# Layer 1 of a two-layer encoder trunk: the merge of the head groups goes by way of DRAM instead of transposes, and two sets of operands start at other addresses

## The chip, the cores and the metric

The kernel runs on one core of one Trainium2 chip. The metric is the device time of one execution in microseconds (us); it is measured several times, and the median is given. TensorE (PE) multiplies and transposes, VectorE (DVE) and ScalarE (ACT) compute elementwise, GpSimd (POOL) does a little elementwise work, and SyncE (SP) issues most of the loads.

## What is computed

The input is one sequence of 512 tokens with 1024 numbers each. Two layers follow each other, each an attention and a SwiGLU FFN with RMSNorm ahead of both, and a last RMSNorm. Layer 0 has windowed attention with grouped queries and is touched by the change only in the address of two buffers. Layer 1 is dilated attention: three groups of 16 heads look at their own token's neighbourhood at steps of 1, 4 and 16, and for every head the three outputs are added with weights that come from the three softmax denominators.

```python
DILATED_GROUPS = ((128, 1), (512, 4), (2048, 16))
BLOCK_B = 64

def dilated_mixture_attention(h, w_qkv, w_out):
    b, s, _ = h.shape
    qkv = (h @ w_qkv).reshape(b, s, N_GROUPS_B, 3, H_B, HEAD_DIM)
    slopes = alibi_slopes(H_B)[:, None]
    outs, lses = [], []
    for gi, (win, dil) in enumerate(DILATED_GROUPS):
        q = to_residue(qkv[:, :, gi, 0], dil)[:, :, :, None]
        k = to_residue(qkv[:, :, gi, 1], dil)
        v = to_residue(qkv[:, :, gi, 2], dil)
        o, lse = banded_attention(q, k, v, slopes, dil, win // (2 * dil), BLOCK_B)
        outs.append(from_residue(o[:, :, :, 0], b, dil))
        lses.append(from_residue(lse[:, :, :, 0], b, dil))
    wts = jax.nn.softmax(jnp.stack(lses), axis=0)
    o = jnp.einsum('gbsh,gbshd->bshd', wts, jnp.stack(outs).astype(jnp.float32))
    return o.astype(h.dtype).reshape(b, s, H_B * HEAD_DIM) @ w_out
```

## The kernel before

All values are fp32. For a matmul each operand is split into a high part, rounded for TensorE (names that end in h), and the rest (names that end in l), and `mm3` (L113 to L119) runs three products: high by high, high by low, low by high. Each is a matmul of a 128x128 weight tile with 256 moving columns. The normed input stands feature by token in xh and xl, the attention output in oh and ol, the hidden part of the FFN in ah and al.

**Weights.** `unit` (L161) is a product of all 512 tokens with 128 weight columns: 8 steps of six matmuls. `values` (L190) makes the values of four heads, tokens by columns, with the input as stationary and the weights as moving operand, and its accumulator is named psv. A weight block of 128x1024 comes by a DMA from SP into wraw (L101), and `split` (L91) makes wh on ScalarE (L92) and wl on VectorE (L93). There are three buffers of each (pool wpool).

**Order of the work.** TensorE's order is written by hand (`manual_schedule`). In layer 1 the matmuls of the projections are the filler: `fillers` yields steps of six matmuls, and `weave` puts a given number of them (32, 48 at the first) between the steps of a list which attention returns. The instructions of the other engines are put in order by a scheduler from modelled times, so an instruction that waits holds up all that was put behind it on its engine. PSUM has eight banks: mm 3, sc 2, tp 2, ov 1; a step that asks for a bank waits until its last user is through.

**Layer 1.** Eight head pairs p of two heads follow each other. For each, `attention_a` does group 0 (step 1) and `attention_b` groups 1 and 2 together, by residue class c of four. The queries and keys of group 0 are qa and ka (L585, L595), split into qs, ks and kl (`split_queries`, `split_keys`); those of the next pair are made as filler while this pair's attention_b runs, and its `scores_a` (L639) needs them.

1. `scores_a` makes the scores of four query tiles, and VectorE and ScalarE turn them to weights not yet divided. Per query and head they leave two numbers, minus the maximum and the sum of exponentials, in sta, a tile of 128 queries by 4 tiles by 32 columns of which 4 are used.
2. `merge_turn` (L763) transposes sta on TensorE (L766), and five copies on VectorE (L771) put the statistics into strow in the order of the classes. `merge_back` (L779) transposes strow back with four small transposes (L781) and copies the result to sa (L784): the statistics of the same queries, in the order which attention_b uses.
3. `turn_a` and `weigh_a` transpose the weights (L661) and multiply by the values (L680). The sum goes to acca, 128 (two heads of 64 features) by 512 queries.
4. `scores_b` makes the scores of groups 1 and 2 for two classes at a time (L698), takes the maximum with sa's (L714), the exponentials, and the common denominator. From these comes the share that group 0 has per query and head; L726 spreads it over 64 columns into ew.
5. `turn_b` transposes the weights: the first half on TensorE (L740), the second on VectorE (L743, pt from pr). `merge_rows` (L786) transposes the four parts of ew on TensorE (L790), so that the share stands in a row for every feature, and multiplies acca by it (L792).
6. `weigh_b` multiplies by the values (L753), adds acca (L759, tmp) and splits into oh and ol for this pair.

At the end `out_part` runs the output projection from oh and ol: five of its eight blocks run alone behind the last attention, after three that serve as the last filler.

In these loops, `bank("tp")` serves the transposes of turn_a, turn_b and of all three merge functions. GpSimd has no instruction in layer 1 from the first operands to the end of attention.

Of the kernel before, what the change touches and what calls it, by code (L numbers as in the profile page):

```python
# [12 lines left out]
OP = mybir.AluOpType  # L13
# [51 lines left out]
def trunk(ctx, tc, xT, gains, sink, tabs, qsc, wunits, wv, outT):  # L65
# [29 lines left out]
    def weight_tiles():  # L95
        return (wpool.tile([128, 1024], F32, name="wraw"), wpool.tile([128, 1024], F32R, name="wh"),
                wpool.tile([128, 1024], F32R, name="wl"))

    def load(tiles, src, cols):
        raw, wh, wl = (t[:, cols] for t in tiles)  # L100
        nc.sync.dma_start(raw, src[:, cols])  # L101
        split(wh, wl, raw)

    def chunks(tiles, shape):
        n = int(np.prod(shape))
        return [t[:, :n].rearrange("p (a b) -> p a b", a=shape[0]) for t in tiles[1:]]

    def load_unit(src, shape):
        tiles = weight_tiles()
        load(tiles, src, slice(0, int(np.prod(shape))))  # L110
        return chunks(tiles, shape)
# [77 lines left out]
    def values(i, col, hi, lo, out, tags="mm mm mm mm"):  # L189


        def gen():
            w = [load_unit(wv[2 * i + k], (4, 256)) for k in range(2)]
# [104 lines left out]
    with tc.tile_pool(name="l0", bufs=2) as pool:  # L298
        v0 = pool.tile([128, 4, 256], F32, name="v0", bufs=1)
        pool.tile([128, 96], F32, name="align", bufs=1)  # L300
# [260 lines left out]
    with tc.tile_pool(name="l1", bufs=2) as pool:  # L561
        pool.tile([128, 96], F32, name="align", bufs=1)
# [4 lines left out]

        stats = [pool.tile([128, 4, 32], F32, name=f"sta{k}", bufs=1) for k in range(2)]
        for t in stats:
            nc.gpsimd.memset(t, 0.0)  # L570
# [51 lines left out]
        def scores_a(p, ts):  # L622
            if ts[0] == 0:
                st["sta", p] = stats[p % 2]
# [62 lines left out]
        def scores_b(p, cs):  # L687
# [28 lines left out]
            for c in cs:  # L716
                for a in range(2):
# [6 lines left out]
            ew = pool.tile([128, 2, 2, 64], F32, name="ew", bufs=3)  # L724
            st["ew", p, cs[0]] = ew
            nc.vector.tensor_tensor(ew, e[:, :, :, None].to_broadcast([128, 2, 2, 64]),  # L726
                                    den[:, :, :, None].to_broadcast([128, 2, 2, 64]), op=OP.mult)
# [35 lines left out]
        def merge_turn(p):  # L763

            ps = bank("tp", "stt")
            nc.tensor.transpose(ps[:, :128], st["sta", p].rearrange("p t e -> p (t e)"), ident)  # L766
            row = st["row", p] = pool.tile([4, S], F32, name="strow", bufs=1)
            by_class = row.rearrange("p (m i) -> p i m", m=16)

            def put(i, n, src):  # L770
                nc.vector.tensor_copy(by_class[:, i:i + n], src.rearrange("p (i m) -> p i m", m=16))  # L771

            put(0, 4, ps[:4, 64:128])
# [187 lines left out]
```

## Time and profile before

| what | value |
|---|---|
| median of 3 runs | 1470.56 us (1470.53 to 1471.1) |
| the profiled execution | 1470.28 us |
| its span, first to last instruction | 1468.5 us |
| granted TensorE clock, mean | 0.994 |
| matmuls and transposes (PE) | 12820 |
| VectorE's and ScalarE's instructions | 1400 and 1126 |
| DMA | 128.29 MB, mean 87 GB/s |

The span is the profiler's time from the first to the last instruction of one execution; the execution as a whole is 1.8 us longer. Lines of the page's groups read: line, engine, operation, output from inputs, shape and count, then busy time and the mean ns of one, then the idle time ahead of it and what ended most of it. Lines of the timeline read: start and duration in us, engine, line, operation, output from inputs, shape, and how many alike; in brackets the wait ahead of it, and on what. A matmul's duration runs to its modelled end, so matmuls overlap, and what one costs TensorE is the distance between two starts. Lines of stretches read: from and to, their length, then busy time and count of TensorE, of the weight loads, VectorE, ScalarE and GpSimd, then the granted clock, the DMA engines' busy share and GB/s.

### The profile page before, as it was taken

To read this page: it belongs to the slowest core of one execution; us is meant where nothing else is said; L and a number is where in the kernel's file an instruction comes from. 1 tells how busy PE (TensorE), PEld (TensorE's weight loads), DVE (VectorE), ACT (ScalarE), POOL (GpSimd) and SP (SyncE) were. 2 spreads that over 40 slices of the span, in tenths; PEclk is the share of its full clock that TensorE was granted. 3 is DMA by queue.
4 is the path that set the end of the run, shared out by engine and by line. 5 is a ranking of instruction groups with operands and counts; after the bars stand their busy time and mean duration, and the time that the engine had idled before them with its cause. 6 is when DMAs were issued, how large, how long until landed. Compare 5 with 4: busy or idle time off the path is not lost.

```text
span 1468.5 us, 29609 instructions
## 1 busy us (share of the span) xinstructions
PE 1451.2 (99%) x12820; PEld 1424.3 (97%) x12820; DVE 732.6 (50%) x1400; ACT 612.0 (42%) x1126; POOL 110.7 (8%) x152
## 2 busy tenths in 40 slices
PE   8999999999999999999999999999999999999997
PEld 8988999999999999999999999999999999999997
DVE  6776544444443345346556556556464444443223
ACT  6776433322323335444545536536343332332221
POOL 4334200000000010000000000000030000000111
PEclk9999999999999999999999999999999999999998
DMA  6110222233223232312212122122132233232321
GB/s 202 58 59 15 87 101 87 101 101 98 93 91 105 94 100 77 109 58 91 82 59 87 65 80 84 61 87 73 44 116 90 98 101 101 87 101 91 97 102 58
DMA packets 38450, 128.29 MB, mean 87 GB/s; under 512 B 4528, under 2 KB 6832, under 8 KB 38320
## 3 DMA queue, kind: packets, MB, share of 16 engines
q1 hardware_dynamic: 36832, 125.08, 25.6%
q8 instruction: 100, 1.64, 0.4%
q10 hardware_dynamic: 1488, 1.33, 0.3%
q14 instruction: 30, 0.25, 0.1%
HBM read 124.29 MB, written 2.10 MB: 86 GB/s over the span
## 4 chain that ended last, share of the span: by engine, by line
PE 94%; DVE 2%; ACT 2%; issue 0%; DMA 0%; POOL 0%; DVEq 0%; SPq 0%; ACTq 0%; POOLq 0%
PE mm L118 52%; PE sc L118 16%; PE psv L118 9%; PE tp L118 8%; PE sc L698 1%; PE ov L379 1%; PE sc L639 1%; PE sc L140 1%; PE ov L753 1%; PE tp L365 1%; PE tp L661 1%; PE ov L680 1%; PE tp L740 0%; DVE wl L93 0%; DVE x L475 0%
## 5 line engine op out<-in xcount | busy, mean ns | idle before, releaser
L92 ACT ACTIVATE wh<-wraw 128x1024 fp32r<-128x1024 f32 (+3 forms) x239 | 247.0, 1035 | 599.3 <-PE mm L118 253.8
L93 DVE TENSOR_TENSOR wl<-wraw,wh 128x1024 fp32r<-128x1024 f32 (+3 forms) x239 | 290.5, 1216 | 201.4 <-ACT wh L92 200.7
L118 PE MATMUL mm<-xh,wh 128*128 128x256 f32 x1632 | 330.7, 284 | 0.9 <-ACT xh L217 0.9
L118 PE MATMUL mm<-xh,wl 128*128 128x256 f32 x1632 | 321.2, 278 | 1.4 <-DVE wl L93 1.4
L118 PE MATMUL mm<-xl,wh 128*128 128x256 f32 x1632 | 321.3, 278 | 0.3 <-DVE xl L218 0.3
L118 PEld LDWEIGHTS mm<-xh,wh 128*128 128x128 f32 x1632 | 248.2, 189 | 6.7 <-issue 4.8
L118 PEld LDWEIGHTS mm<-xh,wl 128*128 128x128 f32 x1632 | 248.2, 189 | 1.9 <-DVE wl L93 1.8
L118 PEld LDWEIGHTS mm<-xl,wh 128*128 128x128 f32 x1632 | 248.3, 189 | 0.9 <-DVE xl L218 0.7
L232 POOL TENSOR_TENSOR ssum<-ssum,tmp 128x512 f32<-128x512 f32 x34 | 54.7, 1609 | 991.3 <-ACT tmp L228 976.7
L118 PE MATMUL psv<-wh,xh 128*128 128x256 f32 x288 | 82.6, 287 | 0.0
L118 PE MATMUL psv<-wh,xl 128*128 128x256 f32 x288 | 80.3, 279 | 0.0
L118 PE MATMUL psv<-wl,xh 128*128 128x256 f32 x288 | 80.2, 279 | 0.0
L118 PE MATMUL mm<-al,wh 128*128 128x256 f32 x374 | 74.8, 276 | 0.0
L118 PE MATMUL mm<-ah,wh 128*128 128x256 f32 x374 | 74.8, 277 | 0.0
L118 PE MATMUL mm<-ah,wl 128*128 128x256 f32 x374 | 74.6, 276 | 0.0
L118 PE MATMUL tp<-xh,wh 128*128 128x256 f32 x352 | 68.8, 277 | 0.0
L118 PE MATMUL tp<-xh,wl 128*128 128x256 f32 x352 | 68.8, 276 | 0.0
L118 PE MATMUL sc<-xh,wh 128*128 128x256 f32 x352 | 68.7, 277 | 0.0
L118 PE MATMUL tp<-xl,wh 128*128 128x256 f32 x352 | 68.6, 276 | 0.0
L118 PE MATMUL sc<-xh,wl 128*128 128x256 f32 x352 | 68.6, 276 | 0.0
L118 PE MATMUL sc<-xl,wh 128*128 128x256 f32 x352 | 68.5, 276 | 0.0
L118 PE MATMUL sc<-al,wh 128*128 128x256 f32 x330 | 66.1, 276 | 0.0
(175 smaller groups left out, 2726.4 us busy)
## 6 DMA issues: line engine op xcount, KB each, us to landing
wraw<-wunits SPq DMA_DIRECT2D x192, 512.0 KB, 3.2
wraw<-wv SPq DMA_DIRECT2D x26, 512.0 KB, 3.2
wraw<-wunits SPq DMA_DIRECT2D x16, 384.0 KB, 2.9
x<-xT SPq DMA_DIRECT2D x8, 256.0 KB, 5.2
wraw<-wunits SPq DMA_DIRECT2D x3, 256.0 KB, 5.4
outT<-x ACTq DMA_DIRECT2D x2, 384.0 KB, 2.7
tab<-tabs SPq DMA_DIRECT2D x1, 512.0 KB, 5.7
outT<-x ACTq DMA_DIRECT2D x2, 256.0 KB, 2.2
```

What stands on the lines that cost most here:

```text
L92: nc.scalar.activation(out_h, src, AF.Copy)
L93: nc.vector.tensor_tensor(out_l, src, out_h.bitcast(F32), op=OP.subtract)
L118: nc.tensor.matmul(out[:, cols], a, b[:, cols], start=first and k == 0 and c == 0, stop=last and k == 2, skip_group_check=True)
L140: nc.tensor.matmul(outs[a], qp[a][:, qc], k[a][:, kc], start=first and k is kp, stop=k is low, skip_group_check=True)
L232: nc.gpsimd.tensor_tensor(norm["sum"], norm["sum"], sq, op=OP.add)
L365: nc.tensor.transpose(tp[:, 256 * hf + 128 * i:256 * hf + 128 * i + 128], st["pr"][:, 2 * i + hf, 128 * kb:128 * kb + 128], ident)
L379: nc.tensor.matmul(ov[64 * hf:64 * hf + 64, :256], v0[:, k0 // 128 + kb, vs], st["pt", kb][:, 256 * hf:256 * hf + 256], start=(kb == 0), s ...
L639: nc.tensor.matmul(out, qk["qs", p][a][:, 128 * t:128 * t + 128], kp[k], start=t == ts[0] and k == 0, stop=k == 1, skip_group_check=True)
L661: nc.tensor.transpose(tp[:, (nb * a + kb) * 128:(nb * a + kb) * 128 + 128], st["pr", p, ts][:, a, o + 128 * kb:o + 128 * kb + 128], ident)
L680: nc.tensor.matmul(ov[rows, 128 * t - 64:128 * t + 64], v[:, t - 1 + kb, vs], pt[:, 256 * a + 128 * kb:256 * a + 128 * kb + 128], start=Fa ...
L698: nc.tensor.matmul(ps[a][:, o:o + 128], qk["q", p, 1 + g][rows, cols], qk["k", p, 1 + g][rows, cols], start=(o == 0), stop=True, skip_grou ...
L753: nc.tensor.matmul(ov[rows, 128 * c:128 * c + 128], vals[p // 2, 1 + g][:, c, hv + 64 * a:hv + 64 * a + 64], pts[g][:, 256 * a + 128 * (c ...
```

## The change

It has two parts.

**The merge of the groups.** `merge_turn` and `merge_back` are replaced by `merge`: GpSimd stores sta (now 128x4x4, a new tile for each pair) to a DRAM tile stats of 512 queries and 64 more, which hold the first 64 again, by two DMAs, and loads sa from it by four, each 32 partitions, in the order of the classes. L726's wide product becomes a small one, 128x4; after each half of scores_b GpSimd stores the shares of both heads to a DRAM tile (two DMAs with pieces of 4 bytes, L727 after the change), and `merge_rows` loads each head's row of 512 shares to 64 partitions (two DMAs, L780 after the change). The multiplication with acca is now `weigh_rows` (L783 after the change), which reads SBUF rather than PSUM and is called one pause later. The transposes on TensorE and the copies on VectorE go. The step at which `merge` is called stands ahead of the first turn rather than behind the second.

**Addresses.** The filler tile align is 64 floats rather than 96 in both layers, so oh and ol start 128 bytes earlier, at 448 rather than 64 modulo 512 bytes. The tiles wh and wl are 1152 columns wide rather than 1024, and the weights of values start 96 floats into them, at 384 rather than 0 modulo 512; other weights stay at 0.

```diff
     def weight_tiles():
-        return (wpool.tile([128, 1024], F32, name="wraw"), wpool.tile([128, 1024], F32R, name="wh"),
-                wpool.tile([128, 1024], F32R, name="wl"))
-
-    def load(tiles, src, cols):
-        raw, wh, wl = (t[:, cols] for t in tiles)
+        return (wpool.tile([128, 1024], F32, name="wraw"), wpool.tile([128, 1152], F32R, name="wh"),
+                wpool.tile([128, 1152], F32R, name="wl"))
+
+    def load(tiles, src, cols, at=0):
+
+        raw, wh, wl = tiles[0][:, cols], *[t[:, at + cols.start:at + cols.stop] for t in tiles[1:]]
...
-            w = [load_unit(wv[2 * i + k], (4, 256)) for k in range(2)]
+            w = [load_unit(wv[2 * i + k], (4, 256), 96) for k in range(2)]
...
-        pool.tile([128, 96], F32, name="align", bufs=1)
+        pool.tile([128, 64], F32, name="align", bufs=1)
...
-
-        stats = [pool.tile([128, 4, 32], F32, name=f"sta{k}", bufs=1) for k in range(2)]
-        for t in stats:
-            nc.gpsimd.memset(t, 0.0)
+        dram = ctx.enter_context(tc.tile_pool(name="dram", bufs=2, space=bass.MemoryType.DRAM))
...
-                st["sta", p] = stats[p % 2]
+
+                st["sta", p] = pool.tile([128, 4, 4], F32, name="sta")
...
-            ew = pool.tile([128, 2, 2, 64], F32, name="ew", bufs=3)
-            st["ew", p, cs[0]] = ew
-            nc.vector.tensor_tensor(ew, e[:, :, :, None].to_broadcast([128, 2, 2, 64]),
-                                    den[:, :, :, None].to_broadcast([128, 2, 2, 64]), op=OP.mult)
+            if cs[0] == 0:
+                st["shares", p] = dram.tile([2, S], F32, name="shares")
+            nc.vector.tensor_tensor(e, e, den, op=OP.mult)
+            for a in range(2):
+                nc.gpsimd.dma_start(st["shares", p][a].rearrange("(c p) -> p c", c=4)[:, both], e[:, :, a])
...
-        def merge_turn(p):
...
+        def merge(p):
+
+
+            sta = st["sta", p]
+            by_query = dram.tile([S + 64, 4], F32, name="stats")
+            nc.gpsimd.dma_start(by_query[:S].rearrange("(t q) e -> q t e", t=4), sta)
+            nc.gpsimd.dma_start(by_query[S:], sta[:64, 0, :])
 
             sa = st["sa", p] = pool.tile([128, 4, 4], F32, name="sa")
-            nc.vector.tensor_copy(sa.rearrange("p c e -> p (c e)"), ps[:, :16])
+            by_class = by_query[64:].rearrange("(m c i) e -> i m c e", c=4, i=4)
+            for i in range(4):
+                nc.gpsimd.dma_start(sa[32 * i:32 * i + 32], by_class[i])
 
         def merge_rows(p):
 
-            pr = bank("tp", "rrow")
-            for c in range(4):
-                nc.tensor.transpose(pr[:, 128 * c:128 * c + 128],
-                                    st["ew", p, c // 2 * 2][:, c % 2].rearrange("p a d -> p (a d)"), ident)
-            nc.vector.tensor_tensor(st["acca", p], pr, st["acca", p], op=OP.mult)
+            rows = st["rows", p] = pool.tile([128, S], F32, name="rows", bufs=1)
+            for a in range(2):
+                nc.gpsimd.dma_start(rows[HALVES[a]], st["shares", p][a:a + 1].to_broadcast([64, S]))
+
+        def weigh_rows(p):
+            nc.vector.tensor_tensor(st["acca", p], st["rows", p], st["acca", p], op=OP.mult)
...
             return [lambda: scores_a(p, (0, 1)), 0, lambda: scores_a(p, (2, 3)), 0,
-                    lambda: turn((0, 1), 0), lambda: turn((0, 1), 1), lambda: merge_turn(p),
-                    lambda: turn((2, 3), 2), 0, lambda: turn((2, 3), 3), lambda: merge_back(p), 0, weigh]
+                    lambda: merge(p), lambda: turn((0, 1), 0), lambda: turn((0, 1), 1),
+                    lambda: turn((2, 3), 2), 0, lambda: turn((2, 3), 3), 0, 0, weigh]
...
             return [lambda: scores_b(p, (0, 1)), pauses[0], 0, lambda: scores_b(p, (2, 3)), pauses[1], 0, 0,
-                    lambda: turn((0, 1)), pauses[2], 0, 0, lambda: turn((2, 3)), pauses[3], lambda: merge_rows(p),
-                    pauses[4], 0, weigh]
+                    lambda: turn((0, 1)), pauses[2], 0, 0, lambda: turn((2, 3)), pauses[3],
+                    lambda: merge_rows(p), pauses[4], lambda: weigh_rows(p), weigh]
```

Three places show how the instructions move. The first is VectorE in the second half of pair 2, behind the last product that makes the shares. Names: wl is a weight block's low part, pt the transposed weights of attention, qa, qs and ka the next pair's queries and keys, mm their accumulator. Before:

```order
L726 TENSOR_TENSOR ew<-mb 128x256
L93 TENSOR_TENSOR wl<-wraw,wh 128x1024
L743 STREAM_TRANSPOSE pt_8922<-pr_8768 128x512
L93 TENSOR_TENSOR wl<-wraw,wh 128x1024
L585 SCALAR_TENSOR_TENSOR qa<-mm,qs_sb,rb 128x16x28
L585 SCALAR_TENSOR_TENSOR qa<-mm,qs_sb,rb 128x16x4
L743 STREAM_TRANSPOSE pt_8982<-pr_8833 128x512
L93 TENSOR_TENSOR wl<-wraw,wh 128x1024
L128 TENSOR_TENSOR qs_8975<-qa,qs_8975 64x512
L128 TENSOR_TENSOR qs_8976<-qa,qs_8976 64x512
L792 TENSOR_TENSOR acca<-rrow,acca 128x512
L595 TENSOR_TENSOR ka<-mm,rb 128x16x32
```

The same place after:

```order
L725 TENSOR_TENSOR mb<-mb 128x4
L93 TENSOR_TENSOR wl<-wraw,wh 128x1024
L743 STREAM_TRANSPOSE pt_8907<-pr_8750 128x512
L93 TENSOR_TENSOR wl<-wraw,wh 128x1024
L783 TENSOR_TENSOR acca<-rows,acca 128x512
L583 SCALAR_TENSOR_TENSOR qa<-mm,qs_sb,rb 128x16x28
L583 SCALAR_TENSOR_TENSOR qa<-mm,qs_sb,rb 128x16x4
L743 STREAM_TRANSPOSE pt_8967<-pr_8817 128x512
L93 TENSOR_TENSOR wl<-wraw,wh 128x1024
L129 TENSOR_TENSOR qs_8960<-qa,qs_8960 64x512
L129 TENSOR_TENSOR qs_8961<-qa,qs_8961 64x512
L593 TENSOR_TENSOR ka<-mm,rb 128x16x32
```

The product with acca (L792, now L783) has moved from behind the next pair's qs to ahead of its qa; pairs 0, 4 and 6 are like this one. In pairs 1, 3 and 5 it has moved from behind the second transpose (L743) to ahead of it.

The second place is VectorE at the end of the last pair, 7, where ol is what the output projection waits for. Before:

```order
L726 TENSOR_TENSOR ew<-mb 128x256
L743 STREAM_TRANSPOSE pt_12387<-pr_12279 128x512
L792 TENSOR_TENSOR acca<-rrow,acca 128x512
L759 TENSOR_TENSOR tmp<-ov,acca 128x16x32
L93 TENSOR_TENSOR ol<-tmp,oh 128x512
```

The same place after:

```order
L725 TENSOR_TENSOR mb<-mb 128x4
L743 STREAM_TRANSPOSE pt_12347<-pr_12238 128x512
L783 TENSOR_TENSOR acca<-rows,acca 128x512
L759 TENSOR_TENSOR tmp<-ov,acca 128x16x32
L93 TENSOR_TENSOR ol<-tmp,oh 128x512
```

The order is the same here; what differs is that L783 takes the rows that a DMA lands where L792 took those that TensorE transposed. The third place is GpSimd's queue in every pair after the change; before, it holds nothing there.

```order
L769 DMA stats<-sta 64x4
L768 DMA stats<-sta 128x4x4
L774 DMA sa<-stats 32x4x4 x4
L727 DMA shares<-mb 128x2x1 x4
L780 DMA rows<-shares 64x512 x2
```

All twelve DMAs of a pair stand in this one queue, each issued behind the ones above it. On TensorE 72 transposes go, nine for each pair: one of L766, four of L781 and four of L790.

26 lines of the change are left out of this document (6 added, 20 removed).

## The prediction

> **What bounds the kernel now.** I read the page first, then TensorE's groups by form, then stretches of equal length, then single places on the timelines of TensorE and VectorE, and at last the DMA issues.
>
> The page's span and busy times:
>
> ```profile
> span 1468.5 us, 29609 instructions
> PE 1451.2 (99%) x12820; PEld 1424.3 (97%) x12820; DVE 732.6 (50%) x1400; ACT 612.0 (42%) x1126; POOL 110.7 (8%) x152
> ```
>
> TensorE is busy for 99% of the span. So work that leaves TensorE comes off the time one for one, VectorE's savings (50% busy) buy nothing by themselves, and a new wait costs only where TensorE comes to stand behind it. Start, sizes of the queues and the end are untouched; I look at layer 1, and at the matmuls whose operands change their address.
>
> **Part 1: 72 transposes leave TensorE.** Each of the eight head pairs loses one transpose of the statistics (L766), four small ones back (L781) and four of the shares (L790). What one visit costs is read from the starts of the matmuls around it. TensorE's timeline, column one the start, at the three places of pair 3:
>
> ```profile
> 801.54 0.39 PE L118 MATMUL mm<-xh,wl 128*128 128x256 f32 x2
> 801.77 0.27 PE L766 MATMUL stt<-ident,sta 128*128 128x128 f32 x1
> 801.80 0.48 PE L118 MATMUL mm<-xh,wh 128*128 128x256 f32 x2
> 802.12 0.40 PE L118 MATMUL mm<-xl,wh 128*128 128x256 f32 x2
> ...
> 809.35 0.39 PE L118 MATMUL mm<-xl,wh 128*128 128x256 f32 x2
> 809.58 0.39 PE L118 MATMUL mm<-xh,wl 128*128 128x256 f32 x2
> 809.90 0.40 PE L781 MATMUL stc<-ident,strow 4*128 4x4 f32 x4
> 810.23 0.50 PE L118 MATMUL mm<-xh,wh 128*128 128x256 f32 x2
> 810.57 0.40 PE L118 MATMUL mm<-xl,wh 128*128 128x256 f32 x2
> ...
> 837.97 0.28 PE L118 MATMUL psv<-wh,xl 128*128 128x256 f32 x1
> 838.09 0.60 PE L790 MATMUL rrow<-ident,ew 128*128 128x128 f32 x4
> 838.45 0.36 PE L118 MATMUL psv<-wh,xh 128*128 128x256 f32 x1
> 838.65 0.28 PE L118 MATMUL psv<-wl,xh 128*128 128x256 f32 x1
> ```
>
> Undisturbed, a pair of matmuls starts 0.23 us after the last (809.35 to 809.58), one alone 0.115 us. So the statistics' turn costs 802.12 - 801.54 - 0.46 = 0.12 us, the way back 810.57 - 809.58 - 0.46 = 0.53 us, the shares 838.65 - 837.97 - 0.23 = 0.45 us. Eight times 1.10 is **8.8 us** off. VectorE's copies L771 and L784 and the wide product L726 go as well; nothing waits for VectorE there, so they count zero.
>
> **Part 2: addresses.** In the built programs oh and ol start at 64 modulo 512 bytes before and at 448 after, the values' weights wh and wl at 0 and at 384; xh and xl stay at 448, other weights at 0, ah and al at 192. Take the difference of moving minus stationary operand: oh over weights goes from 64 to 448; value weights over xh from 64 (0 - 448) to 448; value weights over oh stays at 448; xh over weights is 448 and ah over weights 192 throughout. Groups by form, with mean ns of one before the bar's end, and counts in four stretches:
>
> ```profile
> L118 PE MATMUL mm<-xl,wh 128*128 128x256 f32 x1632 | 321.3, 278 | 0.3 <-DVE xl L218 0.3
> L118 PE MATMUL psv<-wh,xl 128*128 128x256 f32 x288 | 80.3, 279 | 0.0
> L118 PE MATMUL mm<-al,wh 128*128 128x256 f32 x374 | 74.8, 276 | 0.0
> L118 PE MATMUL mm<-ol,wh 128*128 128x256 f32 x256 | 50.7, 279 | 0.0
> ```
>
> ```profile
> 29.00:37.00 8.00, 8.00 (x73) 8.00 (x72) 5.85 (x8) 6.47 (x11) 0.00 (x0) 1.00 0.20 68
> 1072.00:1092.00 20.00, 20.00 (x172) 20.00 (x171) 11.70 (x14) 8.83 (x12) 5.93 (x4) 1.00 0.37 129
> 1110.00:1130.00 20.00, 20.00 (x179) 20.00 (x178) 9.35 (x13) 6.66 (x9) 0.00 (x0) 1.00 0.30 104
> 566.00:586.00 20.00, 20.00 (x179) 20.00 (x178) 6.43 (x8) 11.59 (x19) 0.00 (x0) 1.00 0.21 65
> ```
>
> In 20 us, layer 1's output projection (oh over weights, difference 64, from 1072) fits 172 matmuls; the FFN (xh over weights, 1110) and the values of group 0 (weights over oh, 566), both at 448, fit 179. That is 116.3 against 111.7 ns, 4.6 ns each, at a granted clock of 1.00 in all. The two groups at difference 64 are also those with 279 ns in the list above. One row speaks against: layer 0's values (29 to 37) are at 64 too and run 73 in 8 us, quick. So 64 seems to let the stream fall into a slower step, not to force it. Affected are 3 x 256 = 768 matmuls on oh and ol, and 864 psv less these 96 quick ones, 768. Bounds: zero, and 1536 x 4.6 ns = 7.1 us. The oh ones run mostly undisturbed and I count them fully, 3.5 us. The psv ones stand among attention's breaks, where even the favourable xl group averages 278, between 276 and 279: a third, 1.2 us. Together **4.7 us** off.
>
> The Trainium skill, TensorE: Matmul & The Clock Gate, section Part 2: What happens when you issue a matmul, says that the moving operand and the weight load have read ports of their own, so that loading the next weights takes nothing from the running matmul. By it addresses could not matter and this term would be zero; the 172 against 179 disagree, the row at 29 us agrees.
>
> **Part 3: the way through DRAM.** Per pair GpSimd now issues two stores and four loads for the statistics, and per half of the scores two stores of 4-byte pieces (L727), then two loads of the shares (L780). No GpSimd DMA is in the trace. Let R be the time from the end of the second small product (in the place of L726) to the landing of both rows: two legs of store, then load, each with a second issue behind the first. Nearest rows, KB and us to landing, and one issue on SP:
>
> ```profile
> outT<-x SPq DMA_DIRECT2D x2, 128.0 KB, 1.8
> g_sb<-gains ACTq DMA_DIRECT2D x1, 20.0 KB, 3.0
> qs_sb<-qsc SPq DMA_DIRECT2D x1, 8.0 KB, 4.6
> sink_sb<-sink SPq DMA_DIRECT2D x1, 8.0 KB, 5.1
> 1.18 0.42 SPq L101 DMA_DIRECT2D wraw<-wunits  x1
> ```
>
> A leg is 0.4 + 1.8 = 2.2 us at least and 0.4 + 5.1 = 5.5 us at most by these: R from 4.4 to 11.0. qs_sb and sink_sb queued behind the first big loads; g_sb found its queue empty, as a small DMA in layer 1 would, but had one issue and wide pieces. I take 4.0 us a leg, between g_sb and qs_sb with the issue: **R = 8.0**. By the Trainium skill, DMA: Bandwidth & Descriptors, section Anatomy of one DMA — SWDGE (gpsimd) path, a DMA has about 2 us fixed, which would make R an estimated 4 to 6 and the sum about 1457 us; no run here shows it yet.
>
> The statistics are off the path: attention_a's list is woven with 32 steps of six other matmuls, 20 of them behind the merge, so 20 x 6 x 111.7 ns = 13.4 us pass before scores_b needs sa; two stores and four loads take 5.5 + 6.3 = 11.8 us even at the upper bound (two issues more). The shares are different. L783 waits for the rows in VectorE's queue, and all behind it waits too. Three cases.
>
> *Pairs 0, 2, 4, 6.* Behind L783 stand qa, a transpose, weight splits, qs, ka and kl, which the next pair's scores read. Pair 2 on VectorE, ScalarE and TensorE:
>
> ```profile
> 771.83 0.42 DVE L726 TENSOR_TENSOR ew<-mb 128x256 f32<-128x256 f32 x1
> ...
> 778.37 1.17 DVE L585 SCALAR_TENSOR_TENSOR qa<-mm,qs_sb,rb 128x448 f32<-128x448 f32 x2 [1.23 <-PE mm L118]
> ...
> 781.24 1.40 DVE L128 TENSOR_TENSOR qs<-qa,qs 64x512 fp32r<-64x512 f32 x2
> ...
> 784.72 1.08 DVE L595 TENSOR_TENSOR ka<-mm,rb 128x512 f32<-128x512 f32 x1 [1.35 <-PE mm L118]
> ...
> 788.45 1.28 ACT L135 ACTIVATE kl<-kl 64x512 fp32r<-64x512 f32 x2
> ...
> 789.79 0.39 PE L639 MATMUL sc<-kl,qs 128*128 128x256 f32 x1
> ```
>
> L783 (0.69) must start by 778.37 - 0.69 = 777.68 to cost nothing, R = 5.4. From qa on the queue is tight to qs's end (782.64); then 2.1 us are free before ka. From ka over kl to TensorE at 789.79 there is 0.1 us. So TensorE stands for R - 7.6 at each: 0.4 us, times four 1.6.
>
> *Pairs 1, 3, 5.* Behind L783 stands the second transpose, which the weighing reads. Pair 3:
>
> ```profile
> 831.19 0.42 DVE L726 TENSOR_TENSOR ew<-mb 128x256 f32<-128x256 f32 x1
> ...
> 842.83 1.97 PE L753 MATMUL ov<-pt,v 128*64 128x128 f32 x32
> ```
>
> The place of L726 ends at 831.61, the second half of the 32 matmuls begins at about 843.7. Less 0.45 for the shares' transposes, now gone, and 0.69 and 0.7 for L783 and the transpose, R up to 10.3 costs nothing.
>
> *Pair 7*, where few other matmuls are left:
>
> ```profile
> 1054.52 0.42 DVE L726 TENSOR_TENSOR ew<-mb 128x256 f32<-128x256 f32 x1
> 1060.46 1.03 DVE L759 TENSOR_TENSOR tmp<-ov,acca 128x512 f32<-128x512 f32 x1 [2.63 <-PE ov L753]
> 1062.19 0.69 DVE L93 TENSOR_TENSOR ol<-tmp,oh 128x512 fp32r<-128x512 f32 x1 [0.70 <-ACT oh L92]
> ...
> 1063.39 0.28 PE L118 MATMUL mm<-ol,wh 128*128 128x256 f32 x1
> ```
>
> From 1054.94 the chain is R, L783 0.7, then L759 to ol's end 2.42; TensorE wants ol at 1063.39 - 0.45 = 1062.94. It stands for R - 4.9 = 3.1 us.
>
> **The sum.** Profiled execution 1470.3 us (span 1468.5 and 1.8 around it; the median of the runs is 1470.56). 1470.3 - 8.8 - 4.7 + 1.6 + 3.1 = **1461.5 us**.
>
> **The rivals.**
>
> *The round trip is slow.* Scattered 4-byte stores take longer than any row here. Loss is (R - 4.9) + 4 (R - 7.6), and above 10.3 another 3 (R - 10.3); the gains are 13.5. They balance at R = 9.8. At the upper bound, 11.0: 6.1 + 13.6 + 2.1 = 21.8, so 1478.6 us. For it: 256 pieces a store, and GpSimd's issue is unseen; against: the DMA engines are 0.20 to 0.37 busy in the four stretches above. 0.15, and 0.10 for R near the balance, 1467.4 to 1473.2.
>
> *Quick round trip*, R under 4.9, nobody waits: 1470.3 - 13.5 = 1456.8 us. 0.10.
>
> *Addresses do nothing*, as the page on TensorE would have it and as layer 0's values run: 1461.5 + 4.7 = 1466.2 us. For it the row at 29 us, against it the other four. 0.10.
>
> **How the numbers follow.** My forecast has 0.55, the rivals 0.15, 0.10, 0.10 and 0.10 as given. The range leaves out the far side of the slow trip and the quickest: with all 7.1 us of addresses and R under 4.9 it is 1454.4; with R at 9.8 to 9.9 it is 1471. So 1454.5 to 1471. What a measurement of this kernel can tell from no change is about 0.2%, 2.9 us. Faster by more: forecast, quick trip, addresses, 0.75; within: 0.10; slower: 0.15.
>
> **What would show it.** Right: rows L766, L781 and L790 gone, psv and mm on oh at 276 to 277 ns and some 178 in 20 us; L759 of pair 7 late, with TensorE idle 3 us before its ol; scores L639 of pairs 1, 3, 5, 7 waiting under 1 us for kl. Wrong: TensorE waiting over 2 us at those scores, any wait of L714 for sa, stretches on oh that still hold 172, or the rows landing outside 4.4 to 11 us.

## The result, and the profile after

The changed kernel takes 1539.3 us (median of three runs, 1538.31 to 1545.65), against 1470.8 us before: a ratio of 1.0481, 95% interval 1.0465 to 1.0496, so 4.8% slower. A fourth run, 1662.75 us at a mean clock of 0.835, is left out of the comparison. The profiled execution took 1545.65 us.

The page's span, busy times, TensorE's and its clock's slices:

```profile
span 1543.8 us, 29595 instructions
PE 1468.4 (95%) x12748; PEld 1437.1 (93%) x12748; DVE 715.7 (46%) x1352; ACT 612.6 (40%) x1126; POOL 169.8 (11%) x246
...
PE   8999999999999999979889897987979999999997
...
PEclk9999999999999999989999898998999999999999
```

TensorE is idle for 1543.8 - 1468.4 = 75.4 us, where it was idle for 17.3. That is 58.1 us of the 75.3 that the span grew. And although it has 72 transposes fewer, it is busy 17.2 us longer. The slices show both in the same place, from 656 us (the first pair's merge) to the end of layer 1's attention: idle tenths, and with them a lower granted clock. The waits of TensorE, engine and line, the line that was waited for, total, times, longest:

```profile
PE ov L753 <- DVE pt L743: 40.2, 7, 6.9
PE mm L119 <- ACT oh L92: 8.0, 1, 8.0
PE sc L638 <- ACT ks L134: 5.8, 4, 1.7
PE sc L638 <- ACT kl L136: 3.5, 4, 0.9
```

Seven pairs wait in the weighing for a transpose of VectorE, four then wait for the next pair's keys, and the last waits for oh. Together 57.5 us. Pair 2, at the place that the prediction showed, on VectorE:

```profile
789.89 0.16 DVE L725 TENSOR_TENSOR mb<-mb 128x4 f32<-128x4 f32 x1
...
793.98 1.23 DVE L93 TENSOR_TENSOR wl<-wraw,wh 128x1024 fp32r<-128x1024 f32 x1 [1.55 <-ACT wh L92]
808.04 0.69 DVE L783 TENSOR_TENSOR acca<-rows,acca 128x512 f32<-128x512 f32 x1 [12.83 <-DMA rows<-shares]
808.65 1.11 DVE L583 SCALAR_TENSOR_TENSOR qa<-mm,qs_sb,rb 128x448 f32<-128x448 f32 x2
809.63 0.70 DVE L743 STREAM_TRANSPOSE pt<-pr 128x512 f32<-128x512 f32 x1
```

L783 stands ahead of qa and of the second transpose (L743), and waits 12.83 us for the rows. On TensorE this is:

```profile
803.43 1.31 PE L753 MATMUL ov<-pt,v 128*64 128x128 f32 x20
810.39 1.55 PE L753 MATMUL ov<-pt,v 128*64 128x128 f32 x12 [5.65 <-DVE pt L743]
811.87 0.80 PE L119 MATMUL mm<-xh,wh 128*128 128x256 f32 x2
812.46 0.63 PE L119 MATMUL mm<-xl,wh 128*128 128x256 f32 x2
812.89 0.63 PE L119 MATMUL mm<-xh,wl 128*128 128x256 f32 x2
...
815.99 0.39 PE L638 MATMUL sc<-ks,qs 128*128 128x256 f32 x1 [1.70 <-ACT ks L134]
817.30 0.58 PE L638 MATMUL sc<-kl,qs 128*128 128x256 f32 x1 [0.92 <-ACT kl L136]
```

The weighing stops after 20 of 32 matmuls. GpSimd's timeline gives the two legs of R:

```profile
790.35 1.45 POOL L727 DMA_DIRECT2D shares<-mb  x2 [3.27 <-DVE mb L725]
800.01 0.55 POOL L780 DMA_DIRECT2D rows<-shares  x1 [8.21 <-DMA shares<-mb]
801.00 0.54 POOL L780 DMA_DIRECT2D rows<-shares  x1 [0.44 <-DMA shares<-mb]
```

The first load is issued 9.7 us after the first store, since it waits for the stores to land, and L783 starts 7.0 us after the second load's issue. Counted from the first store's issue, R is 17.7 us here, and 18.2, 15.8, 17.7, 17.7, 17.9, 15.2, 18.3 and 13.4 in the eight pairs. The DMA issues of the whole program, KB each and median us to landing:

```profile
wraw<-wunits SPq DMA_DIRECT2D x192, 512.0 KB, 3.3
rows<-shares POOLq DMA_DIRECT2D x16, 128.0 KB, 6.9
sa<-stats POOLq DMA_DIRECT2D x32, 2.0 KB, 2.8
shares<-mb POOLq DMA_DIRECT2D x32, 1.0 KB, 11.3
stats<-sta POOLq DMA_DIRECT2D x8, 8.0 KB, 2.5
```

Here lies the loss. A store of shares carries 1 KB and lands in 11.3 us; a store of statistics carries 8 KB, from the same queue, and lands in 2.5. And between 785 and 812 us the loads of weights land in 11.1 us instead of 3.3:

```profile
wraw<-wunits SPq DMA_DIRECT2D x3, 512.0 KB, 11.1
```

The second part of the loss is the clock. Four stretches around pair 2's stall (the third figure from the end is the granted clock):

```profile
790.00:804.00 14.00, 14.00 (x129) 13.87 (x130) 3.12 (x4) 5.49 (x10) 2.53 (x4) 1.00 0.42 53
804.00:812.00 8.00, 2.35 (x27) 1.78 (x23) 3.93 (x6) 2.16 (x3) 0.00 (x0) 0.67 0.22 74
812.00:820.00 8.00, 5.38 (x24) 4.82 (x25) 6.64 (x13) 4.56 (x8) 0.00 (x0) 0.71 0.39 132
820.00:830.00 10.00, 10.00 (x86) 10.00 (x85) 5.58 (x23) 5.95 (x18) 1.32 (x2) 0.98 0.18 56
```

In the stall and behind it the clock is down, and a pair of matmuls takes 0.43 us (812.46 to 812.89 in the rows above) instead of 0.23. In layer 1 the trace has the clock at 0.50 for 78.5 us in spells of 3.4 to 17.1 us, 51.3 of them with TensorE busy. At half the pace that loses 25.6 us of work (an estimate; 0.43 against 0.23 us is a little better than half). The account closes to about a microsecond: 58.1 idle and 25.6 for the clock, less 8.8 for the transposes, is 74.9 of the 75.3 us. It has no room for the 4.7 us of the addresses. The Trainium skill, TensorE: Matmul & The Clock Gate, section Part 1: The HAM clock gate, says that the array falls to half its clock after an idle window of about 3.4 us and takes as long a busy one to recover. This trace agrees with the half clock, with waits of 4.4 to 8.0 us and spells that are multiples of 3.4 us; but the spell in pair 6 lasted 17.1 us, 11.3 of them with TensorE busy, and experiment 3 below shows one beside a wait of only 2.2 us. The prediction didn't use that section.

Only the address term shows a gain, and a loss beside it:

```profile
566.00:586.00 20.00, 20.00 (x172) 20.00 (x171) 5.74 (x7) 10.98 (x18) 0.00 (x0) 1.00 0.17 54
1155.00:1175.00 20.00, 20.00 (x179) 20.00 (x178) 9.31 (x11) 7.39 (x11) 7.15 (x4) 1.00 0.33 110
```

The output projection (from 1155) now fits 179 matmuls in 20 us, as predicted; but the values of group 0 (from 566), which had 179 before and whose operands' difference has not changed, now have 172. The groups that the prediction wanted to see at 276 to 277 ns have not moved from 279:

```profile
L119 PE MATMUL psv<-wh,xl 128*128 128x256 f32 x288 | 80.2, 279 | 0.0
```

### The profile page after: what moved, and what is told of

It reads as the page before. It is cut to its first block, busy times and chain, and to the rows that moved or that the text cites. A ratio compares the mean times of both kernels' runs of the same rounds, so it can differ in the third digit from the quotient of the medians.

```text
span 1543.8 us, 29595 instructions
## 1 busy us (share of the span) xinstructions
PE 1468.4 (95%) x12748; PEld 1437.1 (93%) x12748; DVE 715.7 (46%) x1352; ACT 612.6 (40%) x1126; POOL 169.8 (11%) x246
## 5 line engine op out<-in xcount | busy, mean ns | idle before, releaser
L119 PE MATMUL mm<-xh,wh 128*128 128x256 f32 x1632 | 334.5, 287 | 1.3 <-ACT xh L218 1.3
L119 PE MATMUL mm<-xh,wl 128*128 128x256 f32 x1632 | 325.2, 281 | 1.6 <-DVE wl L93 1.6
L119 PE MATMUL mm<-xl,wh 128*128 128x256 f32 x1632 | 326.1, 282 | 0.6 <-DVE xl L219 0.6
L119 PEld LDWEIGHTS mm<-xh,wh 128*128 128x128 f32 x1632 | 253.7, 193 | 8.2 <-issue 5.9
L119 PEld LDWEIGHTS mm<-xl,wh 128*128 128x128 f32 x1632 | 253.4, 193 | 1.4 <-DVE xl L219 1.4
L119 PEld LDWEIGHTS mm<-xh,wl 128*128 128x128 f32 x1632 | 252.2, 192 | 2.1 <-DVE wl L93 2.1
L119 PE MATMUL sc<-xl,wh 128*128 128x256 f32 x352 | 68.5, 276 | 0.0
```

The lines of the kernel that those rows point to most:

```text
L119: nc.tensor.matmul(out[:, cols], a, b[:, cols], start=first and k == 0 and c == 0, stop=last and k == 2, skip_group_check=True)
```

## The experiments

The theory that these lines suggest is **pieces**: the 4-byte pieces of the shares' stores keep the DMA engines from writing, so that the stores, the loads of weights beside them and the loads of rows behind them are late; VectorE's queue hands this on to TensorE. The rivals: **GpSimd** (its way of issuing DMAs is slow for any DMA), the **statistics**, and the **addresses**.

**1. Addresses alone.** The kernel before with the part of the diff on weight_tiles, load, values and both align tiles.

> The kernel before with the new addresses alone (oh and ol at 448 modulo 512, weights of values at 384), no DRAM way. Theory A, the difference of moving minus stationary address decides (the prediction): 4.7 us off, about 1466. Theory B, the slow step moves from one set of matmuls to another, as the changed kernel shows (172 to 179 in 20 us in the output projection, but 179 to 172 in the values of group 0 and 73 to 71 in 8 us in layer 0's values): 768 matmuls gain 3.5 us, 768 lose as much, 1470 to 1472. Theory C, the address part is itself a cause of the slowdown: over 1480.

Measured: 1468.49 us, ratio 0.9983 (0.9974 to 0.9992), so 2.5 us off (1.2 to 3.8), between the forecasts of theories A and B. The output projection:

```profile
1072.00:1092.00 20.00, 20.00 (x173) 20.00 (x172) 10.44 (x13) 7.86 (x11) 6.87 (x4) 1.00 0.40 121
```

173 matmuls at the new address: the row on which the 3.5 us were built did not move, so theory A's working is wrong even though a gain is there. Nor does the trace place the gain where the prediction looked: layer 1's values begin 1.6 us earlier than before (560.38 against 561.95 us), and from there to the end it is 0.6 us longer. Theory C is out: the addresses are no cause of the slowdown.

**2. Statistics alone by DRAM.** merge instead of merge_turn and merge_back, new lists of attention_a; the shares by transposes and the addresses as before.

> Old addresses; the statistics go by DRAM, the shares by TensorE's transposes as before. Theory A, the statistics' way stands off the path: five of nine transposes of each pair go, 8 x 0.65 = 5.2 us off, 1465.6, and no wait for sa. Theory B, any DMA of GpSimd costs: scores_b waits for sa, over 1475.

Measured: 1465.74 us, ratio 0.9965 (0.9951 to 0.9979), so 5.1 us off, as theory A says; no instruction that reads sa waits for its DMA.

**3. Pieces of 128 bytes.** VectorE turns the shares in blocks of 32 by 32 before they are stored.

```diff
-            nc.vector.tensor_tensor(e, e, den, op=OP.mult)
-            for a in range(2):
-                nc.gpsimd.dma_start(st["shares", p][a].rearrange("(c p) -> p c", c=4)[:, both], e[:, :, a])
+            wide = wides[cs[0] // 2]
+            nc.vector.tensor_tensor(wide[:, 0:4].rearrange("p (c a) -> p c a", a=2), e, den, op=OP.mult)
+            turned = pool.tile([128, 32], F32, name="turned", bufs=3)
+            nc.vector.transpose(turned, wide)
+            for c in range(2):
+                for a in range(2):
+                    nc.gpsimd.dma_start(
+                        st["shares", p][a, 128 * (cs[0] + c):128 * (cs[0] + c) + 128].rearrange("(b i) -> b i", b=4),
+                        turned[2 * c + a::32])
```

> The changed kernel, but the shares of a half are turned on VectorE in blocks of 32 by 32 first, so that a half is stored by 4 DMAs of 4 pieces of 128 bytes, not by 2 of 256 pieces of 4 bytes. Theory A, the 4-byte pieces keep the DMA engines busy: from the first store's issue of the second half to the second load's issue, 9.4 to 14.6 us in the changed kernel, it takes 2.9 us for four issues and about 2.5 to land, 5 to 6; the loads of weights beside it land in 3 to 4 us again; the rows land in 3 us, R is 8 to 10 and the time 1462 to 1474. Theory B, DMAs issued by GpSimd are slow whatever their pieces: four issues instead of two, R stays at 13 to 18 or grows, 1540 or more.

Measured: 1469.22 us, ratio 0.9993 (0.9984 to 1.0002): the whole loss is gone. R is 7.4 to 10.1 us. Its DMA issues:

```profile
wraw<-wunits SPq DMA_DIRECT2D x192, 512.0 KB, 3.3
rows<-shares POOLq DMA_DIRECT2D x16, 128.0 KB, 3.3
shares<-turned POOLq DMA_DIRECT2D x64, 0.5 KB, 1.7
```

Twice as many stores from the same queue, each landing in 1.7 us instead of 11.3: GpSimd is not the cause. What is left are small waits:

```profile
PE sc L641 <- ACT kl L136: 3.2, 7, 0.9
PE mm L119 <- ACT oh L92: 2.2, 1, 2.2
```

The longest wait, at the end of pair 7, is enough for 3.4 us at half the clock:

```profile
1058.00:1066.00 8.00, 5.62 (x32) 5.28 (x32) 6.00 (x9) 5.01 (x8) 0.11 (x1) 0.79 0.07 8
```

(The scheduler also puts the product with acca behind the second transpose here, as in the kernel before. R is read from the issues and doesn't depend on that, but the time does; experiments 7 and 9 keep the changed kernel's order.)

**4. The stores from SP.**

```diff
-                nc.gpsimd.dma_start(st["shares", p][a].rearrange("(c p) -> p c", c=4)[:, both], e[:, :, a])
+                nc.sync.dma_start(st["shares", p][a].rearrange("(c p) -> p c", c=4)[:, both], e[:, :, a])
```

> The changed kernel with the stores of the shares issued by SP instead of GpSimd, 4-byte pieces as before. Theory A, the pieces cost: the first leg stays at 9 to 15 us and the time near 1540 (SP's loads of weights then also queue behind these stores, so up to 1560). Theory B, GpSimd's way of issuing costs: the first leg falls under 5 us, R under 10, the time under 1490.

Measured: 1533.64 us, ratio 1.0427 (1.0408 to 1.0446); the first leg, to the first load's issue, is 8.4 to 12.4 us.

```profile
shares<-mb SPq DMA_DIRECT2D x32, 1.0 KB, 9.6
```

The same stores from another engine's queue are as slow. This and the third run settle the rival GpSimd.

**5. The product on GpSimd.**

```diff
-            nc.vector.tensor_tensor(st["acca", p], st["rows", p], st["acca", p], op=OP.mult)
+            nc.gpsimd.tensor_tensor(st["acca", p], st["rows", p], st["acca", p], op=OP.mult)
```

> The changed kernel with the product of acca and the rows on GpSimd instead of VectorE; 4-byte pieces as before. Theory A, the stall comes through VectorE's queue, where transposes and the next keys stand behind a product that waits for the rows: R stays at 13 to 18 us, but the waits of the weighing (L753) and of the scores for the keys go or fall under 1 us each; what is left is pair 7's tail, about 13.4 - 4.9 + 0.9 for the slower engine = 9.4 us and some 4 us of lower clock behind it: 1473 to 1490. Theory B, the 4-byte stores starve TensorE of weights (they land in 12 us instead of 3): TensorE waits for wl instead, over 1510.

Measured: 1508.73 us, ratio 1.0263 (1.0242 to 1.0284); R 13.6 to 19.0. TensorE's waits:

```profile
PE sc L638 <- DVE sta L649: 17.0, 5, 6.1
PE mm L119 <- ACT oh L92: 8.6, 1, 8.6
```

The waits of the weighing are gone, as theory A says, but the time is above its range. The stall moved one step on in VectorE's queue, to the sum with acca (L759), ahead of the next pair's maxima (pair 1):

```profile
738.70 1.01 DVE L759 TENSOR_TENSOR tmp<-ov,acca 128x512 f32<-128x512 f32 x1 [5.83 <-POOL acca L783]
740.40 0.69 DVE L93 TENSOR_TENSOR ol<-tmp,oh 128x512 fp32r<-128x512 f32 x1 [0.69 <-ACT oh L92]
741.01 0.28 DVE L646 CUSTOM_DVE_ANT_0 pr<-sc,tab 64x128 f32<-64x128 f32 x1
```

So 30.6 of the 68.5 us of loss go with the product's place on VectorE; 38 stay, as long as R is long. TensorE waits 0.8 us for wl in all; theory B, starved of weights, is out.

**6. Half the pieces.** One head's shares are stored, and its row loaded for both.

```diff
-            for a in range(2):
+            for a in range(1):
                 nc.gpsimd.dma_start(st["shares", p][a].rearrange("(c p) -> p c", c=4)[:, both], e[:, :, a])
...
-                nc.gpsimd.dma_start(rows[HALVES[a]], st["shares", p][a:a + 1].to_broadcast([64, S]))
+                nc.gpsimd.dma_start(rows[HALVES[a]], st["shares", p][0:1].to_broadcast([64, S]))
```

> The changed kernel, storing the shares of the first head of each pair only and loading that row for both heads (the second head's own shares are left out): 256 pieces of 4 bytes for a half, not 512. Theory A, each piece costs DMA time: the first leg falls from 9.4 to 14.6 us to about half, 5 to 8, R to 8 to 12, the time to 1470 to 1500. Theory B, the leg is a fixed price of a store under load: R stays at 13 to 18, 1530 or more.

Measured: 1537.77 us, ratio 1.0456 (1.0436 to 1.0475).

```profile
shares<-mb POOLq DMA_DIRECT2D x16, 1.0 KB, 9.9
```

Theory A is wrong in this form: half as many pieces take nearly as long (9.9 against 11.3 us), so the price is not one for each piece. Theory B's numbers came true; whether any store under load costs as much is theory L of the next experiment. Four more runs asked what it is a price of: the width of a piece, the pieces that a store has on each DMA engine, the load on the engines, or pieces that fall into the same 64 bytes of DRAM. Sixteen consecutive 4-byte shares fill 64 bytes.

**7. Pieces of 16 bytes.**

```diff
-            for a in range(2):
-                nc.gpsimd.dma_start(st["shares", p][a].rearrange("(c p) -> p c", c=4)[:, both], e[:, :, a])
+            nc.gpsimd.dma_start(st["shares", p].rearrange("o (h p e) -> (o h) p e", h=2, p=128)[cs[0] // 2],
+                                e.rearrange("p c a -> p (c a)"))
```

> The changed kernel, storing a half's shares as they lie, one DMA of 128 pieces of 16 bytes, and loading 512 consecutive numbers of that for both heads (so the shares stand in the wrong order; the waits are the same). Half the pieces in two stores made no difference, so the count over all stores is not it. Theory P, narrow pieces: those of 4 bytes run one after the other, wider ones hardly; the statistics' pieces of 16 bytes land in 2.5 us. Then the first leg falls from 9 to 15 us to 3 to 5, R to 6 to 9, the time to 1461 to 1475. Theory S, pieces that fall into the same 64 bytes of DRAM wait for each other: 4 instead of 16 in each, 3 to 5 us as well. Theory L, the price is that of a store while weights are loaded, whatever its pieces: 9 us or more, over 1530.

**8. Pieces of 8 bytes.** As above, with `e[:, c, :]` stored for each class c.

> As the kernel sent ahead of it, with two DMAs of 128 pieces of 8 bytes for a half. Theory S, 8 pieces in each 64 bytes instead of 16: the leg falls to half, 5 to 7 us, R to 8 to 11, 1465 to 1500. Theory P with a bound between 4 and 8 bytes: 3 to 5 us like 16 bytes; with a bound between 8 and 16: unchanged but for half the pieces, 8 us or more.

**9. The same 4-byte pieces, 64 bytes apart.** The shares of a head lie 16 floats apart in a DRAM tile that is zero elsewhere.

```diff
-                nc.gpsimd.dma_start(st["shares", p][a].rearrange("(c p) -> p c", c=4)[:, both], e[:, :, a])
+                nc.gpsimd.dma_start(st["shares", p][a].rearrange("(c p k) -> p c k", c=4, k=16)[:, both, 0], e[:, :, a])
...
-                nc.gpsimd.dma_start(rows[HALVES[a]], st["shares", p][a:a + 1].to_broadcast([64, S]))
+                nc.gpsimd.dma_start(rows[HALVES[a]], st["shares", p][a:a + 1, 3840:4352].to_broadcast([64, S]))
```

> The changed kernel, storing the same 4-byte pieces 64 bytes apart in DRAM, and loading 512 consecutive numbers there, most of them zeros (so most shares are left out; the waits are the same). Theory S, the pieces of the same 64 bytes wait for each other: none do now, the first leg falls under 5 us, R under 9, the time under 1480. Theory P, each narrow piece costs by itself: the leg stays at 9 to 15 us, 1530 or more.

**10. Four stores of 128 pieces.** One for each class and head.

```diff
-            for a in range(2):
-                nc.gpsimd.dma_start(st["shares", p][a].rearrange("(c p) -> p c", c=4)[:, both], e[:, :, a])
+            for c in range(2):
+                for a in range(2):
+                    nc.gpsimd.dma_start(st["shares", p][a].rearrange("(c p) -> p c", c=4)[:, cs[0] + c:cs[0] + c + 1],
+                                        e[:, c, a:a + 1])
```

> The changed kernel with four stores of 128 pieces of 4 bytes for a half, one for each class and head, instead of two of 256; everything else alike. Theory P, a store's pieces run one after the other on each of the 16 DMA engines, stores beside each other: 8 pieces instead of 16 in a row, the leg falls to 5 to 8 us, of which 1.4 are the two more issues; R 9 to 12, 1475 to 1510. Theory S, each 64 bytes still get 16 pieces: the leg stays at 9 to 15 us or grows by the issues, 1535 to 1560.

Measured, in the order of the runs: the stores' landing of the 16-byte kernel,

```profile
shares<-mb POOLq DMA_DIRECT2D x16, 2.0 KB, 1.7
```

of the 8-byte kernel,

```profile
shares<-mb POOLq DMA_DIRECT2D x32, 1.0 KB, 4.1
```

of the kernel with its pieces apart,

```profile
rows<-apart POOLq DMA_DIRECT2D x16, 128.0 KB, 3.1
...
apart<-mb POOLq DMA_DIRECT2D x32, 1.0 KB, 2.0
```

and of the kernel with four stores:

```profile
shares<-mb POOLq DMA_DIRECT2D x64, 0.5 KB, 13.6
```

| kernel | pieces in 64 bytes | store lands, us | R, us | time, us | ratio (interval) |
|---|---|---|---|---|---|
| changed | 16 of 4 B | 11.3 | 13.4 to 18.3 | 1539.3 | 1.0481 (1.0465 to 1.0496) |
| four stores | 16 of 4 B | 13.6 | 13.2 to 22.1 | 1550.58 | 1.0539 (1.0508 to 1.0570) |
| 8 bytes | 8 of 8 B | 4.1 | 8.3 to 12.0 | 1487.16 | 1.0108 (1.0079 to 1.0137) |
| 16 bytes | 4 of 16 B | 1.7 | 5.9 to 8.3 | 1462.75 | 0.9941 (0.9918 to 0.9964) |
| 64 bytes apart | 1 of 4 B | 2.0 | 6.5 to 8.4 | 1461.31 | 0.9937 (0.9915 to 0.9960) |

Theory L is out: beside the same loads the 16-byte kernel's store lands in 1.7 us. The 8-byte kernel alone would not decide: its first leg, 3.7 to 5.1 us, is under theory S's 5 to 7 and suits a bound by width as well. The kernel with its pieces apart decides. It has the same stores, queue, count and width of pieces as the changed one, the same order on VectorE, and only other addresses in DRAM: its stores land in 2.0 us, R is 6.5 to 8.4, and TensorE waits 1.3 us, at the end of pair 7. So neither width nor count is the price, but how many pieces of a store fall into the same 64 bytes (64 is the spacing that was tried; whether the true block is smaller or larger, and whether the wider spread itself helps, was not, and why they are slow together is not shown). With four stores of half the pieces nothing falls, as theory S says and P denies. (Not all else is alike there: the scheduler puts the product behind the second transpose again, and TensorE's longest waits, 11.8 us, are for the next pair's keys.) The weights' loads were late by the same cause: beside spaced stores, between 760 and 785 us, they land in 3.3 us again:

```profile
wraw<-wunits SPq DMA_DIRECT2D x4, 512.0 KB, 3.3
```

**11, 12. A version that beats both.** Statistics by DRAM, shares in pieces of 128 bytes as in experiment 3, the product on GpSimd as in 5, and for pair 7, where nothing covers R, the shares by transposes as before; once with the new addresses, once with the old.

> New addresses, statistics by DRAM, shares stored in pieces of 128 bytes, the product with acca on GpSimd, and in pair 7 shares by TensorE's transposes as before. If theory A holds and no wait is left, 8 x 0.65 + 7 x 0.45 = 8.4 us of transposes go, and the addresses give what they gave alone, 2.1 to 2.5: about 1460 (1458 to 1463). If something else in the DRAM way costs time, 1466 or more.

> The same as the kernel sent with it, with the old addresses: 8.4 us off, about 1462 (1461 to 1465). If the addresses are worth what the prediction said, 4.7 us more than with the new ones; if they are worth nothing, the same within 1 us.

Measured: 1460.27 us, ratio 0.993 (0.9917 to 0.9943), with the new addresses, and 1463.14 us, ratio 0.9945 (0.9932 to 0.9958), with the old. The forecasts were 1460 and 1462. The 2.9 us between the two are not clear of noise: the ratios are 0.0015 apart, and each is good to 0.0013. TensorE's longest wait from the start of layer 1's attention through the output projection is 0.7 us with either. The output projection, with the new addresses,

```profile
1062.00:1082.00 20.00, 20.00 (x172) 20.00 (x172) 11.88 (x14) 8.92 (x12) 5.83 (x4) 1.00 0.41 133
```

and with the old:

```profile
1062.00:1082.00 20.00, 20.00 (x179) 20.00 (x178) 12.72 (x15) 8.91 (x12) 6.67 (x5) 1.00 0.40 133
```

**13, 14. Each address by itself.** The kernel before with `pool.tile([128, 64], ...)` for align alone, and with the values' weights at 96 floats alone.

> The kernel before with oh and ol at 448 instead of 64 modulo 512, the weights of values at 0 as before, no DRAM way. The prediction's term for it is 3.5 us off (1467), by 172 to 179 matmuls in 20 us of the output projection. With both addresses changed alone, 2.5 us went but that stretch stayed at 173. If the gain hangs on these buffers all the same: 1468; if it hangs on the values' weights or on the wider tiles: 1470.6 within 0.7.

> The kernel before with the weights of values at 384 instead of 0 modulo 512 in tiles of 1152 columns, oh and ol as before, no DRAM way. The prediction's term for it is 1.2 us off (1469.4). If the 2.5 us of both addresses hang on these: 1468; if they hang on oh and ol: 1470.6 within 0.7.

Measured: oh and ol alone 1471.96 us, ratio 1.0008 (0.9999 to 1.0017); the values' weights alone 1471.56 us, ratio 1.0005 (0.9996 to 1.0014). Neither gains anything by itself. The output projection with oh and ol alone at 448:

```profile
1074.00:1094.00 20.00, 20.00 (x179) 20.00 (x179) 12.70 (x15) 8.91 (x12) 6.62 (x5) 1.00 0.40 132
```

At 64 it is 172 before and 179 in experiment 12; at 448 it is 173 and 172 in experiments 1 and 11, and 179 in the changed kernel and in this one. So the slow step of 116 ns exists, and it comes and goes whatever that address is. One execution of each kernel was profiled, so whether it changes from kernel to kernel or from one execution to the next is not known.

## Why the prediction was wrong

**R: the step that failed.** "A leg is 0.4 + 1.8 = 2.2 us at least and 0.4 + 5.1 = 5.5 us at most by these: R from 4.4 to 11.0". The rows that gave these ends are transfers in pieces of 64 bytes or more (8 KB over 128 partitions is 64 bytes each), and the upper end was treated as an end, though no row of the trace showed a store of 4-byte pieces. R was 13.4 to 18.3 us, counted from the first store's issue; from the end of the product, where the prediction starts it, it is 0.3 more. Stores that share 64 bytes account for it in both legs: the first took 8.9 to 14.1 us to the first load's issue; the second, 6.2 to 7.3 in even pairs, where the loads of rows run beside weights that are late by the same stores. Where the pieces stand apart, R is 6.5 to 8.4, and the taken 8.0 would have held. The rival "the round trip is slow" had named scattered 4-byte stores, and was then capped at the same 11.0 us and given 0.15.

What the Trainium skill, DMA: Bandwidth & Descriptors, section Anatomy of one DMA — SWDGE (gpsimd) path, says, about 2 us fixed for a DMA, agrees with the stores of 16 bytes (1.7) and with those apart (2.0), and is far off for those packed closely (11.3). The Trainium skill, DMA: Bandwidth & Descriptors, section Rules for kernel authors, warns that an access with a non-contiguous last dimension becomes one descriptor for each element and should be rearranged. Experiment 9 stores as many elements and is quick, so the number of elements is not the reason here; following the advice would have helped all the same.

**Who waits: right, with one place missed.** With the measured R the thresholds hold within a microsecond, but for the even pairs. Pairs 1, 3 and 5, R - 10.3: 5.5, 7.4 and 4.9 forecast by it, 5.1, 6.9 and 4.4 measured. Pair 7, R - 4.9: 8.5 against 8.0. Pairs 0, 2, 4 and 6, R - 7.6: 10.1 to 10.7 against 8.2 to 8.4; there I had followed the queue to kl alone, and the transpose behind qa stops the weighing first, so TensorE waits at two places with work between. At R = 6.7 in the kernel with pieces apart, pair 7 waits 1.3 us (1.8 by the formula) and the even pairs not at all.

**The clock: left out.** 25.6 us, a third of the loss. Each stall was priced at its own length. In waits of 4.4 to 8.0 us and behind them TensorE's clock was halved for 6.8 to 17.1 us a pair; in experiment 3 a wait of 2.2 us was enough for a spell of 3.4.

**Transposes: right.** 0.65 us for the statistics of a pair makes 5.2, and experiment 2 measured 5.1; with seven of eight pairs' shares 8.4, and experiment 12, at the old addresses, stands 7.5 below its kernel before. In the traces layer 1's attention, from the last matmul of the values on oh to the last weighing, takes 454.2 us before, 449.9 in experiment 2, 446.7 in experiment 12 and, with all 72 transposes gone and no stall in that stretch, 445.0 in experiment 9: 4.4, 7.6 and 9.2 less, for 5.2, 8.4 and 8.8 forecast. That the statistics' way is off the path was right too.

**Addresses: the working was wrong, and what is left of the size is unclear.** 4.7 us were forecast; both together gave 2.5 (1.2 to 3.8) in experiment 1, 2.9 not clear of noise in 11 against 12, and each alone nothing. The difference of the operands' addresses does not decide the slow step, since the same difference was seen slow and quick. The row at 29 us, which spoke against it, deserved more weight than the groups' means (and the stretches shown against it are three, not four); it is itself 71 in experiment 2, where layer 0 is the kernel before's, instead of 73. Whether addresses do nothing, as the rival has it, rests on experiment 1 alone, whose trace does not show its gain at the places that were priced. What decides the step is open.

With R right and all else as it stood, the stalls would have been put at 8.5 in pair 7, 41.7 in the four even pairs and 17.8 in the three odd ones, 68.0 us, and the time at 1470.3 - 13.5 + 68.0 = 1524.8; with 25.6 for the clock it is 1550.4, where the profiled execution took 1545.65. So R is the step that turns a gain into a loss, and the clock a term that was put at nothing.

## What to carry to other kernels

A store whose 4-byte pieces lie side by side in DRAM took more than five times as long here as the same pieces spaced apart (11.3 against 2.0 us), and held up the loads of weights beside it; turn such data first, so that a piece is 16 bytes or more, or space the pieces. Where no row shows a kind of transfer, the rows of other kinds are no upper bound for it. When a wait may stop TensorE for several microseconds, price the lower clock behind it as well, and see what stands behind the waiting instruction in its queue: moving that instruction to another engine moved the stall to the next reader here.

## What the runs showed of the hardware

- Stores in pieces of 4, 8 and 16 bytes that fill the same 64 bytes of DRAM land in 11.3, 4.1 and 1.7 us; 4-byte pieces 64 bytes apart in 2.0 us. The issuing engine (GpSimd 11.3, SP 9.6) and a second store beside it (9.9 with one, 11.3 with two) change little.
- While such stores are under way, packets of 4 KB of the weights' loads, 159 ns in the median, take up to 9.8 us (1.9 at most in the kernel before), and 512 KB land in 11.1 us instead of 3.3.
- In layer 1 of the changed kernel the granted clock was 0.50 for 78.5 us, in spells that are multiples of 3.4 us.
- A stream of 128x256 matmuls runs at 111.7 or 116.3 ns a matmul in the same stretch of the same code at a granted clock of 1.00, from the trace of one kernel to that of the next (20 us of the output projection hold 179 or 172); the operands' addresses that were tried don't decide which.
